# Mixture of softmaxes on one core: one reciprocal and weight product for four heads, four places for exponentials, a hand-written set of waits

## The chip, the cores and the metric

The kernel runs on one core of a Trainium2 chip. The metric is the device time of one execution in microseconds (us), lower is better. A profiled execution gives a span, from the first to the last instruction, and a trace of every instruction and every DMA packet. The engines named here are DVE (VectorE), ACT (ScalarE), POOL (GpSimd) and SP (SyncE, which only issues DMAs in this kernel). ACT can issue DMAs too. TensorE is not used.

## The reference

```python
def reference(logits, prior):            # logits [32, 128, 4, 4096], prior [32, 128, 4], float32
    prior_probs = np.exp(prior - prior.max(axis=-1, keepdims=True))
    prior_probs = prior_probs / prior_probs.sum(axis=-1, keepdims=True)
    softmax = np.exp(logits - logits.max(axis=-1, keepdims=True))
    softmax = softmax / softmax.sum(axis=-1, keepdims=True)
    return np.sum(prior_probs[..., None] * softmax, axis=2)   # [32, 128, 4096]
```

There are 4,096 rows (batch times sequence). Each has four heads of 4,096 logits. The result of a row is the sum of the four softmaxes, each weighted by the softmax of the row's four priors. 268 MB of logits are read and 67 MB of results written.

## The kernel before

The rows are cut into 32 units of 128 rows, one row per partition. A unit's logits are 128 x 4 x 4,096 float32: 8 MB in all, 64 KB in each partition. Two such buffers (`ltile`, line 72) take turns, so that unit b + 2 is loaded where unit b was. A load is issued by SP: one DMA of 8 MB for most units, four of 2 MB (one for each head) for unit 0 and the last three (lines 66 to 76).

The prologue (lines 87 to 105) loads the priors, computes their softmax with the rows along the free dimension, and transposes the weights into `pp`, which holds for each partition and unit the four weights.

The loop over units (line 119) does for each of the four heads:

- line 135, ACT: exponential of the head's 4,096 logits, with the sum along the row as a by-product (`dsum`). The exponentials go to one of two buffers, `ebuf`, which take turns; for the last two units they are written in place over the logits. No maximum is subtracted.
- line 144, DVE: reciprocal of the sum (`rden`), 128 x 1.
- head 0, line 146, DVE: `acc` = exponentials times reciprocal times weight, in one operation with two scalars.
- heads 1 to 3, line 151, POOL: `coeff` = reciprocal times weight, 128 x 1; then line 156, DVE: `acc` = exponentials times `coeff` plus `acc`. For the last head of the last unit this is done in two halves, each with its own store.

An `acc` has two buffers of its own (16 KB per partition); in the last two units it lies in the load buffer. The store of unit b - 1 is issued on ACT's queue ahead of the exponentials of unit b (line 129); the stores of the last four units go out on SP's queue after all loads (lines 163 to 168, 161). Each engine works through its own queue in order. A scheduler of the language puts in the waits between engines; a load waits until its buffer's four exponentials are done, and an exponential waits until the add that reads its `ebuf` is done.

Of the kernel before, what the change touches and what calls it, by code (L numbers as in the profile page):

```python
# [1 line left out]

# [4 lines left out]

FP32 = mybir.dt.float32
AF = mybir.ActivationFunctionType
ALU = mybir.AluOpType  # L10
AX = mybir.AxisListType


def early_first_load(nc):

    blocks = nc.main_func.blocks  # L20
    first = next(
        (b, i)
        for b in blocks[1:]
        for i in b.instructions
        if i.engine == mybir.EngineType.SP and i.opcode == "DMACopy"
    )
    block, ins = first
    assert not ins.sync_info.on_wait
    block.instructions.remove(ins)
    at = next(  # L30
        n
        for n, i in enumerate(blocks[0].instructions)
        if i.engine == mybir.EngineType.SP and i.opcode == "Drain"
    )
    blocks[0].instructions.insert(at, ins)


@with_exitstack
def kernel(
    ctx: ExitStack,  # L40
    tc: tile.TileContext,
    logits: bass.AP,
    prior: bass.AP,
    out: bass.AP,
):
    nc = tc.nc
    B, S, H, V = logits.shape
    assert prior.shape == (B, S, H)
    assert out.shape == (B, S, V)
    P = 128  # L50
    J = 2
    R = P * J
    G = B * S // R
    B = G * J
    assert G * R == B * S and G <= 32

    lg = logits.rearrange("b s h v -> (b s) h v").rearrange("(g p j) h v -> g j p h v", p=P, j=J)
    ov = out.rearrange("b s v -> (b s) v").rearrange("(g p j) v -> g j p v", p=P, j=J)
    pv = prior.rearrange("b s h -> (b s) h").rearrange("(g r) h -> g r h", r=R)

    lpool = ctx.enter_context(tc.tile_pool(name="lpool", bufs=2))
    apool = ctx.enter_context(tc.tile_pool(name="apool", bufs=2))
    cpool = ctx.enter_context(tc.tile_pool(name="cpool", bufs=1))


    def pieces(b):
        return 1 if b == 0 or b >= B - 3 else H

    ltiles = {}

    def load(b, eng=nc.sync):
        lt = lpool.tile([P, H, V], FP32, name="ltile")
        n = pieces(b)
        for h in range(0, H, n):
            eng.dma_start(out=lt[:, h : h + n], in_=lg[b // J, b % J, :, h : h + n, :])  # L75
        ltiles[b] = lt

    accs = {}

    def store(b, lo=0, hi=V, eng=nc.sync):  # L80
        eng.dma_start(out=ov[b // J, b % J, :, lo:hi], in_=accs[b][:, lo:hi])

    load(0, eng=nc.sync)
    nc.at_finalize(early_first_load)


    pr = cpool.tile([G, R, H], FP32, name="pr")
    nc.scalar.dma_start(out=pr, in_=pv)
    load(1, eng=nc.sync)
    pn = cpool.tile([32, H, R], FP32, name="pn")  # L90
    nc.gpsimd.memset(pn, 0.0)  # L91
    pmax = cpool.tile([G, R], FP32, name="pmax")
    nc.vector.reduce_max(pmax, pr, axis=AX.X)  # L93
    nc.vector.tensor_sub(pr, pr, pmax.unsqueeze(2).to_broadcast([G, R, H]))  # L94
    nc.scalar.activation(pr, pr, AF.Exp)  # L95
    nc.vector.reduce_sum(pmax, pr, axis=AX.X)  # L96
    nc.vector.reciprocal(pmax, pmax)  # L97
    nc.vector.tensor_mul(  # L98
        pn[0:G].rearrange("g h r -> g r h"), pr, pmax.unsqueeze(2).to_broadcast([G, R, H])
    )  # L100
    pq = pn.rearrange("g h (p j) -> g j h p", j=J)

    pp = cpool.tile([P, J, H, 32], FP32, name="pp")
    for t in range(P // 32):
        nc.vector.transpose(pp[32 * t : 32 * (t + 1)], pq[:, :, :, 32 * t : 32 * (t + 1)])  # L105

    NCHUNK = 2


    dsum = cpool.tile([P, B * H], FP32, name="dsum")  # L110
    rden = cpool.tile([P, B * H], FP32, name="rden")
    coeff = cpool.tile([P, B * H], FP32, name="coeff")


    ebuf = cpool.tile([P, 2, V], FP32, name="ebuf")

    exps = []

    for b in range(B):
        last = b == B - 1  # L120
        inplace = b >= B - 2
        lt = ltiles.pop(b)
        if not inplace:
            accs[b] = apool.tile([P, V], FP32, name="acc")
        else:
            accs[b] = lt[:, 0]
        acc = accs[b]
        if 0 < b < B - 3:
            store(b - 1, eng=nc.scalar)
        for h in range(H):  # L130
            split = last and h == H - 1
            i = b * H + h
            col = slice(i, i + 1)
            et = lt[:, h] if inplace else ebuf[:, h % 2]
            ex = nc.scalar.activation(et, lt[:, h], AF.Exp, accum_out=dsum[:, col])  # L135
            if h == 0:
                tc.keep_in_program_order(ex)


            if not inplace:  # L140
                if len(exps) >= 2:
                    tc.declare_no_dep(ex.ins, exps[-2], reason="covered by the sum")
                exps.append(ex.ins)
            nc.vector.reciprocal(rden[:, col], dsum[:, col])  # L144
            if h == 0:
                nc.vector.tensor_scalar(  # L146
                    out=acc, in0=et, scalar1=rden[:, col], scalar2=pp[:, b % J, h, b // J : b // J + 1],
                    op0=ALU.mult, op1=ALU.mult,
                )
                continue  # L150
            nc.gpsimd.tensor_mul(coeff[:, col], rden[:, col], pp[:, b % J, h, b // J : b // J + 1])  # L151
            n = NCHUNK if split else 1
            w = V // n
            for c in range(n):
                cs = slice(c * w, (c + 1) * w)
                nc.vector.scalar_tensor_tensor(  # L156
                    out=acc[:, cs], in0=et[:, cs], scalar=coeff[:, col], in1=acc[:, cs],
                    op0=ALU.mult, op1=ALU.add,
                )
                if split:  # L160
                    store(b, c * w, (c + 1) * w)
        if b + 2 < B:
            load(b + 2)
        if b == B - 3:
            store(b - 1)
            store(b)
        elif b == B - 2:
            store(b)


# [1 line left out]
_INS = ['logits', 'prior']  # L172
_OUTS = [((32, 128, 4096), 'float32')]


# [23 lines left out]
```

The softmax here doesn't subtract the row's maximum and nothing guards it: scores larger than these inputs give would overflow.

## Time and profile before

| What | Value |
|---|---|
| Median of 4 runs | 782.81 us (782.76 to 782.86) |
| The profiled execution | 782.86 us, span 780.7 us |
| DVE busy | 531.4 us, 68% of the span, 266 instructions |
| ACT busy | 470.2 us, 60%, 258 instructions |
| POOL busy | 19.3 us, 2%, 101 instructions |
| Exponential, line 135 | 120 + 8 of 3,608 ns |
| First head's product, line 146 | 30 + 2 of about 2,413 ns |
| Add, line 156 | 90 of 4,484 ns, and 7 in the last two units |
| Reciprocal, line 144 | 128 of 160 ns |
| Weight product on POOL, line 151 | 96 of 190 ns |
| Chain that ended last | DMA of loads 66%, ACT 14%, DVE 10% |

The page of a profile lists the busy time of each engine, the span in 40 slices, the DMA queues with the bytes they moved, the chain of work that ended last, and the costliest groups of instructions by line. A group is written with what it writes, an arrow, and what it reads. "q1" is the DMA queue that SP issues to, "q10" that of ACT, "q14" carries blocks of instructions that the engines run. Idle time of an engine that does not set the end costs nothing.

### The profile page before, as it was taken

The numbers are of one execution on the slowest core, as the hardware profiler recorded it, in microseconds if no ns is written. First come the engines' busy times: TensorE is split into PE (matmuls) and PEld (weight loads), VectorE is DVE, ScalarE is ACT, GpSimd is POOL, SyncE is SP. The second block draws the span as 40 slices with busy tenths as digits, with TensorE's granted clock in tenths as the row PEclk, the third lists the DMA queues.
The fourth block names the chain that finished last, engine by engine and source line by source line (L and its number), as shares of the span: only waits on it lengthen the run. The fifth ranks groups of instructions, "written<-read, shape, count | busy, mean of one in ns | idle before, by whom it ended". The sixth has DMA issues, their size and how long they took to land.

```text
span 780.7 us, 853 instructions
## 1 busy us (share of the span) xinstructions
DVE 531.4 (68%) x266; ACT 470.2 (60%) x258; POOL 19.3 (2%) x101
## 2 busy tenths in 40 slices
DVE  5646668656686666866667765677666776668994
ACT  4366555755557655576555765457655567558971
POOL 0000000000000000000000000000000000000000
DMA  9999999999999999999999999999999999999998
GB/s 393 430 423 463 403 470 403 466 408 422 451 415 458 408 462 406 436 438 460 413 436 447 404 459 414 452 421 452 410 458 415 453 416 421 452 413 431 429 429 357
DMA packets 11127, 335.67 MB, mean 430 GB/s; under 512 B 1248, under 2 KB 1248, under 8 KB 1264
## 3 DMA queue, kind: packets, MB, share of 16 engines
q1 hardware_dynamic: 7056, 276.83, 82.2%
q10 hardware_dynamic: 4064, 58.79, 17.6%
q14 instruction: 7, 0.06, 0.0%
HBM read 268.50 MB, written 67.11 MB: 430 GB/s over the span
## 4 chain that ended last, share of the span: by engine, by line
DMA 66%; ACT 14%; DVE 10%; issue 7%; POOL 0%; SPq 0%; DVEq 0%; POOLq 0%; ACTq 0%
DMA ltile<-in_logits_dram 66%; ACT ebuf L135 14%; DVE acc L156 9%; DVE ltile L156 1%; POOL coeff L151 0%; SPq L75 0%; DVE rden L144 0%; DVEq L194 0%; DVE ltile L146 0%; POOLq L194 0%; ACTq L135 0%
## 5 line engine op out<-in xcount | busy, mean ns | idle before, releaser
L135 ACT ACTIVATE ebuf<-ltile 128x4096 f32<-128x4096 f32 x120 | 433.0, 3608 | 281.8 <-DMA ltile<-in_logits_dram 235.1
L156 DVE SCALAR_TENSOR_TENSOR acc<-ebuf,coeff,acc 128x4096 f32<-128x4096 f32 x90 | 403.6, 4484 | 27.3 <-POOL coeff L151 27.3
L144 DVE RECIPROCAL rden<-dsum 128x1 f32<-128x1 f32 x128 | 20.4, 160 | 201.3 <-ACT ebuf L135 201.3
L146 DVE TENSOR_SCALAR acc<-ebuf,rden,pp 128x4096 f32<-128x4096 f32 x30 | 72.4, 2413 | 1.1
L151 POOL TENSOR_TENSOR coeff<-rden,pp 128x1 f32<-128x1 f32 x96 | 18.2, 190 | 746.4 <-DVE rden L144 746.4
L135 ACT ACTIVATE ltile<-ltile 128x4096 f32<-128x4096 f32 x8 | 28.9, 3609 | 4.2 <-DMA ltile<-in_logits_dram 4.2
L156 DVE SCALAR_TENSOR_TENSOR ltile<-ltile,coeff 128x4096 f32<-128x4096 f32 (+1 forms) x7 | 27.0, 3874 | 1.8 <-POOL coeff L151 1.8
L135 ACT ACTIVATION_READ_ACCUMULATOR ebuf<-ltile 128x1 f32 x120 | 22.4, 186 | 0.0
L93 DVE TENSOR_REDUCE pmax<-pr 16x256 f32<-16x1024 f32 x1 | 1.2, 1207 | 6.6 <-DMA pr<-in_prior_dram 6.6
L95 ACT ACTIVATE pr<-pr 16x1024 f32<-16x1024 f32 x1 | 1.1, 1055 | 6.6 <-DVE pr L94 6.6
L146 DVE TENSOR_SCALAR ltile<-ltile,rden,pp 128x4096 f32<-128x4096 f32 x2 | 4.8, 2414 | 0.1
L98 DVE TENSOR_TENSOR pn<-pr,pmax 16x1024 f32<-16x1024 f32 x1 | 1.9, 1943 | 0.1
L95 ACT ACT_TABLE_LOAD x1 | 1.3, 1283 | 1.2 <-PEq L183 1.2
L96 DVE TENSOR_REDUCE pmax<-pr 16x256 f32<-16x1024 f32 x1 | 1.2, 1207 | 1.1 <-ACT pr L95 1.1
L105 DVE STREAM_TRANSPOSE pp<-pn 32x256 f32<-32x256 f32 x4 | 1.7, 436 | 0.1
L97 DVE RECIPROCAL pmax<-pmax 16x256 f32<-16x256 f32 x1 | 1.7, 1741 | 0.0
L135 ACT ACTIVATION_READ_ACCUMULATOR ltile<-ltile 128x1 f32 x8 | 1.5, 187 | 0.0
L94 DVE TENSOR_TENSOR pr<-pr,pmax 16x1024 f32<-16x1024 f32 x1 | 1.2, 1211 | 0.0
L91 POOL MEMSET pn<- 32x1024 f32 x1 | 0.9, 941 | 0.3 <-POOLq L183 0.3
L183 POOL MEMSET const-float32-0.0<- 128x1 f32 x1 | 0.1, 103 | 0.2 <-issue 0.2
L183 POOL MEMSET const-bfloat16-1.0<- 128x1 bf16 x1 | 0.1, 106 | 0.0
L183 POOL MEMSET const-uint8-127<- 128x1 uint8 x1 | 0.1, 106 | 0.0
(1 smaller groups left out, 0.1 us busy)
## 6 DMA issues: line engine op xcount, KB each, us to landing
out_dram<-acc ACTq DMA_DIRECT2D x28, 2048.0 KB, 29.3
ltile<-in_logits_dram SPq DMA_DIRECT2D x16, 2048.0 KB, 20.2
out_dram<-acc SPq DMA_DIRECT2D x2, 2048.0 KB, 32.9
out_dram<-ltile SPq DMA_DIRECT2D x1, 2048.0 KB, 21.2
out_dram<-ltile SPq DMA_DIRECT2D x2, 1024.0 KB, 8.7
ltile<-in_logits_dram SPq DMA_DIRECT2D x28, 32.3
pr<-in_prior_dram ACTq DMA_DIRECT2D x1, 64.0 KB, 5.8
```

The source lines that it names most:

```text
L93: nc.vector.reduce_max(pmax, pr, axis=AX.X)
L94: nc.vector.tensor_sub(pr, pr, pmax.unsqueeze(2).to_broadcast([G, R, H]))
L95: nc.scalar.activation(pr, pr, AF.Exp)
L96: nc.vector.reduce_sum(pmax, pr, axis=AX.X)
L97: nc.vector.reciprocal(pmax, pmax)
L98: nc.vector.tensor_mul(pn[0:G].rearrange("g h r -> g r h"), pr, pmax.unsqueeze(2).to_broadcast([G, R, H]))
L105: nc.vector.transpose(pp[32 * t : 32 * (t + 1)], pq[:, :, :, 32 * t : 32 * (t + 1)])
L135: ex = nc.scalar.activation(et, lt[:, h], AF.Exp, accum_out=dsum[:, col])
L144: nc.vector.reciprocal(rden[:, col], dsum[:, col])
L146: nc.vector.tensor_scalar(out=acc, in0=et, scalar1=rden[:, col], scalar2=pp[:, b % J, h, b // J : b // J + 1], op0=ALU.mult, op1=ALU.mult,)
L151: nc.gpsimd.tensor_mul(coeff[:, col], rden[:, col], pp[:, b % J, h, b // J : b // J + 1])
L156: nc.vector.scalar_tensor_tensor(out=acc[:, cs], in0=et[:, cs], scalar=coeff[:, col], in1=acc[:, cs], op0=ALU.mult, op1=ALU.add,)
```

## The change

The loop is written anew with an order by hand, and with its waits by hand too. In each unit the four exponentials come first, then one reciprocal of 128 x 4 sums, one POOL product of 128 x 4 weights, and then the four DVE operations. In the last four units this is done for two heads at a time. The exponentials of heads 0 to 3 go to four different places: head 0 in place in the load buffer, head 1 to `ebuf1`, head 2 to `ebuf2` in PSUM, head 3 to `ebuf3`. The first head's product has one scalar, `coeff`, and no longer two. The results lie in `obuf`, two buffers as before.

The waits that `only` keeps in the loop:

- a load of unit u waits for the first DVE operation of unit u - 2 (the four pieces of a late unit: the first piece for that, the others for the exponential of their head);
- an exponential of heads 1 to 3 waits for its load and for the DVE operation of the unit before that read its buffer; the fourth, from unit 4 on, also for the store of unit u - 4;
- the reciprocal waits for the last exponential of its group; the POOL product for the reciprocal and, in the first group of a unit, for the store of unit u - 2, which read the same `obuf`;
- the first DVE operation of a group waits for the product, the others for the one before them;
- a store waits for the last add of its unit.

The store of unit u - 1 now stands on ACT's queue ahead of the fourth exponential of unit u, where it stood ahead of the first. The last four units' stores stay on SP's queue behind the loads. The prologue does what it did.

```diff
-    lpool = ctx.enter_context(tc.tile_pool(name="lpool", bufs=2))
-    apool = ctx.enter_context(tc.tile_pool(name="apool", bufs=2))
...
+    def only(ins, *keep):
+        for k in keep:
+            tc.add_manual_dep(
+                ins.ins,
+                k.ins.name,
+                mybir.DependencyInfo(mybir.DependencyClass.Sync, mybir.DependencyReason.DATA),
+                reason="all that this instruction waits for",
+            )
+        tc.declare_no_dep(
+            ins.ins,
+            group="loop",
+            keep=[k.ins for k in keep] + before.get(ins.ins.engine, []),
+            reason="covered by the waits that are kept",
+        )
...
+    ltile = cpool.tile([P, 2, H, V], FP32, name="ltile")
...
+            if u >= 2:
+                only(ld, adds[u - 2, 0] if h == 0 else exps[u - 2, h])
+            else:
+                only(ld)
...
+    def store(u, acc, eng, lo=0, hi=V):
+        st = eng.dma_start(out=ov[u // J, u % J, :, lo:hi], in_=acc[:, lo:hi])
+        stores[u] = only(st, adds[u, H - 1])
...
-    ebuf = cpool.tile([P, 2, V], FP32, name="ebuf")
+    ebuf1 = cpool.tile([P, V], FP32, name="ebuf1")
+    ebuf2 = psum.tile([P, V], FP32, name="ebuf2")
+    ebuf3 = cpool.tile([P, V], FP32, name="ebuf3")
+    obuf = cpool.tile([P, 2, V], FP32, name="obuf")
...
+        for u in range(U):
+            bufd = u < U - 2
+            lt = ltile[:, u % 2]
+            acc = obuf[:, u % 2] if bufd else lt[:, 0]
+            es = (lt[:, 0], ebuf1, ebuf2, ebuf3) if bufd else [lt[:, h] for h in range(H)]
...
+            def exp(h, *keep):
...
+                keep = (loads[u, h],) + keep
+                if bufd and h and u:
+                    keep += (adds[u - 1, h],)
+                exps[u, h] = only(ex, *keep)
+
+            def weigh(h, n, *keep):
+                rc = nc.vector.reciprocal(rden[:, u, h : h + n], dsum[:, u, h : h + n])
+                only(rc, exps[u, h + n - 1])
+                mul = nc.gpsimd.tensor_mul(
+                    coeff[:, u, h : h + n], rden[:, u, h : h + n], ppu[:, h : h + n]
+                )
+                return only(mul, rc, *keep)
+
+            def add(h, mul, lo=0, hi=V):
+                if h == 0:
+                    st = nc.vector.tensor_scalar(
+                        out=acc[:, lo:hi], in0=es[h][:, lo:hi], scalar1=coeff[:, u, h : h + 1],
+                        scalar2=None, op0=ALU.mult,
+                    )
+                    adds[u, h] = only(st, mul)
+                else:
+                    st = nc.vector.scalar_tensor_tensor(
+                        out=acc[:, lo:hi], in0=es[h][:, lo:hi], scalar=coeff[:, u, h : h + 1],
+                        in1=acc[:, lo:hi], op0=ALU.mult, op1=ALU.add,
+                    )
+                    adds[u, h] = only(st, mul, adds[u, h - 1])
+
+            free = (stores[u - 2],) if bufd and u >= 2 else ()
+
+            m = H if u < U - 4 else 2
+            for h in range(H):
+                late = h == H - 1 and 4 <= u < U - 3
+                if h == H - 1 and 0 < u < U - 3:
+                    store(u - 1, obuf[:, (u - 1) % 2], nc.scalar)
+                exp(h, *((stores[u - 4],) if late else ()))
+                if (h + 1) % m:
+                    continue
+                g = h + 1 - m
+                mul = weigh(g, m, *(free if g == 0 else ()))
+                for k in range(g, h + 1):
+                    n = 2 if u == U - 1 and k == H - 1 else 1
+                    w = V // n
+                    for c in range(n):
+                        add(k, mul, c * w, (c + 1) * w)
+                        if n > 1:
+                            store(u, acc, nc.sync, c * w, (c + 1) * w)
+            if u + 2 < U:
+                load(u + 2)
```

## The prediction

> **What bounds the kernel now.** I read the page's slices and queues first, then a table of windows over the span, then the waits, then the chain of one unit, and last the tail on the timeline.
>
> ```profile
> DMA  9999999999999999999999999999999999999998
> DMA packets 11127, 335.67 MB, mean 430 GB/s; under 512 B 1248, under 2 KB 1248, under 8 KB 1264
> q1 hardware_dynamic: 7056, 276.83, 82.2%
> q10 hardware_dynamic: 4064, 58.79, 17.6%
> q14 instruction: 7, 0.06, 0.0%
> ```
>
> The DMA engines are never under nine tenths before the last slice, and the loads (q1, with the last five stores) and the other stores (q10) fill 99.8% of 16 engines. The windows (us, busy time of DVE, ACT, POOL, clock, DMA share, GB/s) say where the rest is:
>
> ```profile
> 0.00:2.00 2.00, 0.00 (x0) 0.80 (x1) 1.15 (x5) 1.00 0.63 139
> 2.00:10.00 8.00, 2.42 (x2) 1.39 (x2) 0.00 (x0) 1.00 0.98 403
> ...
> 200.00:300.00 100.00, 68.55 (x33) 61.82 (x34) 2.40 (x13) 1.00 1.00 433
> ...
> 772.00:776.00 4.00, 0.00 (x0) 0.00 (x0) 0.00 (x0) 1.00 0.97 410
> 776.00:778.00 2.00, 0.00 (x0) 0.00 (x0) 0.00 (x0) 1.00 0.76 320
> 778.00:780.70 2.70, 0.00 (x0) 0.00 (x0) 0.00 (x0) 1.00 0.07 30
> ```
>
> Idle DMA time is 0.74 us in the first two (0.37 x 2.00), 0.16 in the next eight, 0.12 + 0.48 + 2.51 in the last nine: 4.0 us in all. Between, the transfers run at 433 GB/s whatever the engines do. The bytes are fixed, so 335.67 MB / 433 GB/s = 775.2 us is the floor; no scheduling of DVE, ACT or POOL can win more than the 4.0 us. Of these the opening 0.9 stays (the first load and the prior's load are issued as before), and the packet records put the last packet's end at 779.4 us, so that the final landing and drain, 1.3 us, stay too. What is winnable is 4.0 - 0.9 - 1.3 = 1.8 us: the uneven finish. By the same records 12 of 16 DMA engines end between 777.3 and 777.6 us and the last at 779.4, so 1.8 to 1.9 us after most.
>
> ```profile
> ACT ebuf L135 <- DMA ltile<-in_logits_dram: 235.1, 28, 15.4
> DVE rden L144 <- ACT ebuf L135: 201.3, 57, 13.2
> ACT ebuf L135 <- DVE acc L156: 44.6, 32, 1.4
> ```
>
> ACT waits 235.1 us for loads, which is the bound seen from the engine; the 44.6 us for a free ebuf and all POOL round trips lie under it. One middle unit (13) by the chain of waits (start, us, what), then its store and the next unit on the timeline:
>
> ```profile
> 332.47 7.32 ACT ebuf L135 x4
> 348.32 0.20 ACT ebuf L135
> 348.54 32.29 DMA ltile<-in_logits_dram
> ```
> ```profile
> 354.52 0.34 ACTq L81 DMA_DIRECT2D out_dram<-acc  x1
> 356.65 3.62 ACT L135 ACTIVATE ebuf<-ltile 128x4096 f32<-128x4096 f32 x1 [8.14 <-DMA ltile<-in_logits_dram]
> ```
>
> Call T the start of a unit's first exponential. Units follow at 356.65 - 332.47 = 24.18 us. The load two units on goes out at T + 16.07, 8.1 us before the next unit's data are in, so the load queue has work; the store goes out at T + 22.05.
>
> **The change part by part.** *Reciprocals and weights.* 128 reciprocals of 160 ns become 36, 96 POOL products of 190 ns become 36: 92 x 0.16 = 14.7 us of DVE and 60 x 0.19 = 11.4 us of POOL go, all under the transfers. The wider forms (128x4) have no row; the 16x256 reciprocal at 1,741 ns bounds them above, 160 ns below; I take the lower, being nearer. Worth nothing while the DMA is full; were it not, a unit would lose or win at most 1.6 us.
>
> *Three exponential tiles, one in PSUM, one in place.* ACT no longer stalls 1.42 us a unit: four exponentials take 3.62 + 3 x 3.60 + 0.17 = 14.6 us. A 128x4096 exponential into PSUM and an add that reads PSUM have no row. For the add the same operation from SBUF (4,484 ns) is nearest; below lies the 2,412 ns of TENSOR_SCALAR, above I allow twice 4,484. Taken: 4,484. The exponential in place has a row (3,609, against 3,608); into PSUM I take 3.61 us, with 1.8 and 7.2 as half and double. At 7.2 the load of the next paragraph leaves 3.6 us later, still 3.1 ahead; at 8.97 for the add the store leaves up to 1.6 us later. Both stay hidden in the middle; the tail is rival B.
>
> *The load's release.* Load u+2 now waits for the first add of unit u, which waits for all four sums: 14.6 + 0.03 + 0.47 (reciprocal start to add start, 50.81 to 51.28) + 2.41 = T + 17.5, so 1.4 us later than now and 6.7 us before the next unit.
>
> *The store's place.* The store of u-1 stands before the fourth exponential of u on ACT's queue: T + 3.62 + 2 x 3.60 + 0.1 = T + 10.95 of the next unit, that is 35.1 us after its own T instead of 22.05, 13 us later. Behind it on ACT waits only that fourth exponential. The adds of u-1 end at 14.6 + 0.5 + 2.41 + 3 x 4.48 = T + 31.0, before 35.1, so it hardly waits. But POOL's product of u now waits for the landing of store u-2 (obuf has two halves). Issue to landing is 29.3 us (median), so T - 24.18 + 10.95 + 29.3 = T + 16.1, 1.3 us after the sums would allow; the add then ends and the load goes out at T + 16.1 + 0.2 + 2.4 = 18.7, 5.5 us ahead. Behind that product on POOL is nothing until the next unit; on DVE the four adds, which then end at T + 32.2, still under 35.1. The work that hides all this is the other queue: in steady state a store is always in transit, and if the load queue runs dry for a moment the store goes faster. What one queue loses the other gets. Cost 0.
>
> A rule bears on this. The Trainium skill, "DMA: Bandwidth & Descriptors" (Queues, rings and completion order), says that a DMA engine takes packets from its queues in turn. One 16 KB store packet per 64 KB load packet would make a store of 8 packets per engine last as long as a load, a whole period of 24.2 us, however early it is issued. That speaks against putting it later. By the rule its landing would be 24.2 us plus the way in and out, at best T + 11, the product would not wait and the lead would be 6.7 us; by the row above it is 5.5.
>
> *The start.* Load 2 went out at 28.08 us; now after the four sums of unit 0 and its first add, about 30.5 us by the same durations. Load 1 occupies the queue until 42.5 (packet records): cost 0. The first store goes from 34.1 to about 54 us; until then the loads have the engines alone.
>
> *The tail.* Here a term is on the path.
>
> ```profile
> 760.38 3.62 ACT L135 ACTIVATE ltile<-ltile 128x4096 f32<-128x4096 f32 x1 [1.16 <-DMA ltile<-in_logits_dram]
> 761.46 4.48 DVE L156 SCALAR_TENSOR_TENSOR ltile<-ltile,coeff 128x4096 f32<-128x4096 f32 x1 [0.30 <-POOL coeff L151]
> 766.32 4.62 DVE L156 SCALAR_TENSOR_TENSOR ltile<-ltile,coeff 128x2048 f32<-128x2048 f32 x2 [0.30 <-POOL coeff L151]
> ```
>
> Now the third head's add runs beside the last exponential. With one weight op for two heads it waits for that exponential's sum: 764.09 + 0.47 = 764.6, add to 769.1, halves to 771.4 and 773.7, against 768.6 and 770.9: 2.75 us later. The packet records show the halves' first packets at 772.44 and 775.28, since earlier stores stand before them in the queue. So 1.0 us and 1.5 us remain from issue to transfer. From issue to first packet the very first load took 1.0 us, the prior's load, behind other packets, 3.8. At 1.0 the queue never runs dry; at 3.8 it is dry for 2.8 us on most DMA engines, but the slowest is 1.9 us behind and feels 0.9. Cost 0 to 0.9; I take 0, the first load's row being the nearer one (same engine and queue).
>
> *Fewer instructions.* The seven q14 packets are instruction blocks. The records show them at 147 to 750 us, each delaying its DMA engine by about 0.65 us; the engine that ends last collected several. Instructions go from 853 to about 853 - 92 - 60 = 701, so perhaps 5.8 blocks rather than 7. Worth 0 (another engine) to 1.8 us (all gone); taken 0.4.
>
> Sum: 780.7 - 0.4 = 780.3 us span. The profiled run took 782.86 for its 780.7, so 2.16 lie around the span: 782.46; the median is 0.05 under that run, hence 782.4.
>
> **Rivals.** *A, slower: the landing of a store closes a loop.* Store u-2 at T + 10.95, landing L later, product and add 2.7, then an unqueued load (8.39 MB and a store's 2.10 MB at 433 GB/s, 24.2 us, and 0.7 to land) over three periods: 3P = 10.95 + L + 2.7 + 24.9. It decides from P = 24.18, that is L = 34.0; each us beyond costs 28/3 = 9.3 us, so 791.7 at L = 35. For it: landings now range from 13.6 to 33.5 us. Against: a load queue that runs dry speeds the store up. *B, slower at the end:* if an add from PSUM takes 8.97 us, units 28 and 29 push DVE back 9 us, the halves end near 777.4 and 779.7, and with 1.0 us to start, 2.4 us for 1 MB and 1.3 to drain the span is 784.4: 786.6. For it: no PSUM row; against: the 4,484 ns add has no fast form to lose. *C, faster:* the uneven finish goes wholly, -1.8: 781.0. For it: fewer instruction blocks; against: some must remain, on some DMA engine.
>
> **How the numbers follow.** A change under 0.2% (1.6 us) I count as none, since that is about what this kernel's measurement tells apart. Forecast 0.80, with own range 781.2 (most of C's gain) to 783.7 (0.9 in the tail). A 0.08, B 0.06, C beyond 0.2% 0.06. The range 781.0 to 784.0 leaves A, B and part of C out. Faster 0.06, same 0.80, slower 0.14.
>
> **What would show it.** DMA share 1.00 and 433 GB/s in every window from 42 to 770 us proves the core of it; ACT's wait for loads grows by the 44.6 us it no longer waits for DVE; stores leave some 13 us later; q14 counts fewer packets; the last half's add ends near 773.7. Wrong: a window in the middle under 1.00 (A), adds from PSUM well over 4.5 us (B).

## The result, and the profile after

The changed kernel takes 781.53 us (median of 41 runs) against 782.69 us (61 runs of the kernel before), a ratio of 0.9987 with a 95% interval of 0.9983 to 0.9992. It is 1.16 us faster, within the 0.2% that the prediction counted as no change. The medians of the spans are 779.8 and 780.6 us, so 0.8 us were won inside the span. The other 0.36 us lie outside it: 1.77 us against about 2.13 us.

First the same page lines of the changed kernel: engines, DMA slices and queues.

```profile
DVE 520.9 (67%) x174; ACT 467.4 (60%) x258; POOL 8.3 (1%) x41
...
DMA  9999999999999999999999999999999999999998
...
q1 hardware_dynamic: 7056, 276.83, 82.3%
q10 hardware_dynamic: 4064, 58.79, 17.6%
q14 instruction: 5, 0.04, 0.0%
```

DVE was busy 10.5 us less and POOL 11.0, and nothing of it shows in the DMA lines: the transfers fill the span as before. Only q14, the blocks of instructions, went from 7 packets to 5. The windows (us, busy DVE, ACT, POOL, clock, DMA share, GB/s) of the changed kernel say the same:

```profile
0.00:2.00 2.00, 0.00 (x0) 0.81 (x1) 1.15 (x5) 1.00 0.60 131
...
200.00:300.00 100.00, 66.64 (x22) 58.02 (x32) 0.97 (x5) 1.00 1.00 433
...
600.00:700.00 100.00, 67.28 (x21) 61.37 (x35) 0.80 (x4) 1.00 0.99 429
...
772.00:776.00 4.00, 0.71 (x1) 0.00 (x0) 0.00 (x0) 1.00 0.95 399
776.00:778.00 2.00, 0.00 (x0) 0.00 (x0) 0.00 (x0) 1.00 0.68 287
778.00:779.70 1.70, 0.00 (x0) 0.00 (x0) 0.00 (x0) 1.00 0.01 5
```

433 GB/s in the middle, as before. The difference is in the last row: before, a few DMA engines still moved bytes after 778 us (share 0.07), now almost none (0.01). By the packet records the last packet ends at 778.37 us instead of 779.40, 1.03 us earlier, which is the whole difference of the two profiled spans (779.7 and 780.7). The waits of the changed kernel:

```profile
POOL coeff L167 <- DVE rden L165: 754.6, 36, 30.0
ACT ltile L156 <- DMA ltile<-in_logits_dram: 285.0, 36, 15.6
DVE rden L165 <- ACT ebuf L156: 224.4, 29, 13.7
```

ACT hardly stalls for an `ebuf` any more (1.2 us in all, 44.6 before) and waits some 50 us longer for its loads (285.0 against 235.1). A stall off the path was turned into waiting for the bound. One middle unit of the changed kernel on the timeline (start, length, what), T = 354.76:

```profile
347.98 13.53 DVE L180 SCALAR_TENSOR_TENSOR obuf<-ebuf,coeff,obuf 128x4096 f32<-128x4096 f32 x3
354.76 3.62 ACT L156 ACTIVATE ltile<-ltile 128x4096 f32<-128x4096 f32 x1 [9.69 <-DMA ltile<-in_logits_dram]
...
358.37 3.60 ACT L156 ACTIVATE ebuf<-ltile 128x4096 f32<-128x4096 f32 x1
361.54 0.34 ACTq L110 DMA_DIRECT2D out_dram<-obuf  x1
...
361.97 3.57 ACT L156 ACTIVATE ebuf<-ltile 128x4096 f32<-128x4096 f32 x1
...
369.30 0.18 DVE L165 RECIPROCAL rden<-dsum 128x4 f32<-128x4 f32 x1 [7.79 <-ACT ebuf L156]
...
372.17 24.48 SPq L97 DMA_DIRECT2D ltile<-in_logits_dram  x2
...
378.91 3.62 ACT L156 ACTIVATE ltile<-ltile 128x4096 f32<-128x4096 f32 x1 [9.65 <-DMA ltile<-in_logits_dram]
```

The load goes out at T + 17.4, 6.7 us ahead of the next unit, as worked out. The store goes out at T + 6.8, when the adds of the unit before have just ended (347.98 + 13.53) and the second exponential still runs, and not at T + 10.95.

The tail of the changed kernel:

```profile
759.36 3.62 ACT L156 ACTIVATE ltile<-ltile 128x4096 f32<-128x4096 f32 x1 [1.18 <-DMA ltile<-in_logits_dram]
...
763.57 9.13 DVE L180 SCALAR_TENSOR_TENSOR ltile<-ltile,coeff 128x4096 f32<-128x4096 f32 x3 [0.31 <-POOL coeff L167]
```

The three DVE operations are the third head's add and the two halves, ending at 772.70. From the last exponential's start that is 13.34 us, where the prediction had 773.7 - 760.4 = 13.3; the exponential itself starts 1.0 us earlier (760.38 before), because its load lands earlier. The slowest DMA engine lags 0.6 us less here, as the table below shows; where the other 0.4 us come from was not traced.

### The profile page after: what moved, and what is told of

It is laid out like the page before. It is cut to its first block, busy times and chain, and to the rows that moved or that the text cites. A ratio compares the mean times of both kernels' runs of the same rounds, so it can differ in the third digit from the quotient of the medians.

```text
span 779.7 us, 670 instructions
## 1 busy us (share of the span) xinstructions
DVE 520.9 (67%) x174; ACT 467.4 (60%) x258; POOL 8.3 (1%) x41
## 4 chain that ended last, share of the span: by engine, by line
DMA 62%; ACT 26%; DVE 8%; issue 2%; POOL 0%; DVEq 0%; SPq 0%; POOLq 0%; ACTq 0%
DMA ltile<-in_logits_dram 62%; ACT ebuf L156 19%; ACT ltile L156 7%; DVE obuf L174 5%; DVE obuf L180 2%; DVE ltile L180 1%; POOL coeff L167 0%; DVE rden L165 0%; DVEq L237 0%; SPq L97 0%; POOLq L237 0%; ACTq L110 0%
## 5 line engine op out<-in xcount | busy, mean ns | idle before, releaser
L180 DVE SCALAR_TENSOR_TENSOR obuf<-ebuf,coeff,obuf 128x4096 f32<-128x4096 f32 x90 | 403.6, 4484 | 3.8 <-POOL coeff L167 0.6
L156 ACT ACTIVATE ebuf<-ltile 128x4096 f32<-128x4096 f32 x90 | 322.9, 3589 | 2.9 <-DMA ltile<-in_logits_dram 1.7
L156 ACT ACTIVATE ltile<-ltile 128x4096 f32<-128x4096 f32 x38 | 137.4, 3616 | 285.0 <-DMA ltile<-in_logits_dram 285.0
L165 DVE RECIPROCAL rden<-dsum 128x4 f32<-128x4 f32 (+1 forms) x36 | 6.3, 174 | 229.3 <-ACT ebuf L156 224.4
L174 DVE TENSOR_SCALAR obuf<-ltile,coeff 128x4096 f32<-128x4096 f32 x30 | 70.6, 2353 | 9.4 <-POOL coeff L167 9.4
L156 ACT ACTIVATION_READ_ACCUMULATOR ebuf<-ltile 128x1 f32 x90 | 16.8, 186 | 0.0
L167 POOL TENSOR_TENSOR coeff<-rden,pp 128x4 f32<-128x4 f32 (+1 forms) x36 | 7.2, 199 | 754.6 <-DVE rden L165 754.6
L156 ACT ACTIVATION_READ_ACCUMULATOR ltile<-ltile 128x1 f32 x38 | 7.1, 186 | 0.0
L174 DVE TENSOR_SCALAR ltile<-ltile,coeff 128x4096 f32<-128x4096 f32 x2 | 4.7, 2352 | 0.6 <-POOL coeff L167 0.6
## 6 DMA issues: line engine op xcount, KB each, us to landing
out_dram<-obuf ACTq DMA_DIRECT2D x28, 2048.0 KB, 29.4
```

The lines of the kernel that those rows point to most:

```text
L156: ex = nc.scalar.activation(es[h], lt[:, h], AF.Exp, accum_out=dsum[:, u, h : h + 1])
L165: rc = nc.vector.reciprocal(rden[:, u, h : h + n], dsum[:, u, h : h + n])
L167: mul = nc.gpsimd.tensor_mul(coeff[:, u, h : h + n], rden[:, u, h : h + n], ppu[:, h : h + n])
L174: st = nc.vector.tensor_scalar(out=acc[:, lo:hi], in0=es[h][:, lo:hi], scalar1=coeff[:, u, h : h + 1], scalar2=None, op0=ALU.mult,)
L180: st = nc.vector.scalar_tensor_tensor(out=acc[:, lo:hi], in0=es[h][:, lo:hi], scalar=coeff[:, u, h : h + 1], in1=acc[:, lo:hi], op0=ALU.mu ...
```

## The experiments

All of them change the changed kernel. Ratios are to the kernel before, run beside them.

**Is it the instruction blocks? Four kernels with more instructions.** m1 takes the weights head by head again:

```diff
-            m = H if u < U - 4 else 2
+            m = 1
...
-                only(ld, adds[u - 2, 0] if h == 0 else exps[u - 2, h])
+                only(ld, *((adds[u - 2, 0], exps[u - 2, h + n - 1]) if h == 0 else (exps[u - 2, h],)))
```

> One reciprocal and one POOL product per head again (92 more of each), all else as in the changed kernel; a load then waits for the first add and the last exponential of its buffer. Theory 'blocks' (the gain is the more even finish of the DMA engines, because fewer instruction blocks are fetched): about 850 instructions as in the kernel before, so q14 moves 7 packets again instead of 5, and the time goes back to 782.2 to 782.8. Rival 'order' (the gain is the new order of stores and loads and the stalls that went): 781.3 to 781.7, as the order stays.

The three others add memsets at the end of a unit (3 on DVE and 2 on POOL in pad_both; 20 on POOL in pad_pool20; 12 on DVE in pad_dve12):

```diff
+    spare = cpool.tile([P, 1024], FP32, name="spare")
...
+            for k in range(12):
+                at = 0 + 12 * u + k
+                only(nc.vector.memset(spare[:, at : at + 1], 0.0))
```

> The changed kernel with three more 128x1 memsets on DVE and two more on POOL in each unit, on a tile that nothing reads: 155 more instructions and nothing else. Theory 'blocks': q14 back to 6 or 7 packets, 782.0 to 782.8. Rival 'order': 781.3 to 781.7.

> The changed kernel with twenty more 128x1 memsets on POOL in each unit, 640 in all, on a tile that nothing reads; POOL is 1% busy, so its time is free. Theory 'blocks': about five more q14 packets, each delaying its DMA engine by 0.65 us; between 781.5 (on engines that end early) and 784.8 (all on the engine that ends last). Rival 'order': 781.3 to 781.7.

> The changed kernel with twelve more 128x1 memsets on DVE in each unit, 384 in all, on a tile that nothing reads; some 1.2 us of DVE in a unit in which it idles 8. Theory 'blocks': about three more q14 packets, 781.5 to 783.5 by the DMA engine that they fall on. Rival 'order': 781.3 to 781.7.

| Kernel | Instructions | q14 packets | Lag of the slowest DMA engine at the last 64 KB packets (about 690 us), us | Span profiled, us | Time, us (ratio, interval) |
|---|---|---|---|---|---|
| before | 853 | 7 | 1.83 | 780.7 | 782.69 |
| changed | 670 | 5 | 1.26 | 779.7 | 781.53 (0.9987, 0.9983 to 0.9992) |
| m1 | 854 | 6 | 2.67 | 780.7 | 782.06 (0.9991, 0.9982 to 1.0) |
| pad_both | 830 | 6 | 1.38 | 779.8 | 781.69 (0.9987, 0.9978 to 0.9996) |
| pad_pool20 | 1310 | 10 | 2.90 | 782.1 | 784.02 (1.0016, 1.0007 to 1.0025) |
| pad_dve12 | 1054 | 8 | 3.72 | 782.2 | 783.95 (1.0014, 1.0006 to 1.0023) |

The lag is read from the packet records: the start of the last of the 16 engines on the last round of 64 KB load packets, less that of the first. m1's lag and profiled span come from an execution of 782.52 us.

m1 lies in neither band, the ranges that the theory and its rival gave. The median of its spans is 780.3 us, between 779.8 of the changed kernel and 780.6 before, so 0.5 of the 0.8 us came back with the instructions; the 0.36 us outside the span did not. pad_both, at 781.69 us with 6 packets, missed the band of the blocks and lies in its rival's. pad_pool20 is inside the band of the blocks, pad_dve12 0.45 us above it. In these two, instructions that nobody waits for, on engines that idle in every unit, cost 2.4 to 2.5 us, so the theory holds in kind. The number of packets alone does not fix the time: eight in pad_dve12 cost as much as ten in pad_pool20.

What counts is which DMA engine they fall on. Almost every packet in the records starts within 5 ns of the end of another, so packets can be followed one behind the other: they fall into 16 rows with 224 load packets each, one row for each DMA engine. A block sets its row back by 0.5 to 0.9 us: 309 ns are its own, and the packet behind it takes longer, up to 3,064 ns for a load packet instead of 2,418. In pad_dve12 a DVE unit has 17 instructions, and the blocks at 84, 264, 449 and 629 us lie 180 to 185 us apart, 7.5 units, or 128 instructions. All four lie in one row and set it back by 0.84 to 0.92 us each; that row ends at 780.84 us, the other 15 by 778.95. In pad_pool20 five blocks (75, 227, 373, 518 and 643 us) lie in one row and set it back by 0.5 to 0.6 us each. So, as far as these records show, the blocks of one compute engine come through one DMA engine, and the DMA engine that is set back most ends last.

The same reading explains the lag of the two kernels. Before, the last row starts its last load packet 1.6 us behind the median row, with two steps of 0.8 us at 147 and 486 us. In the changed kernel it is 1.0 us, with two steps of 0.55 us at 148 and 511 us; a single step of 0.84 us (194 us) falls on another row.

In pad_dve12 the late engine also delays the last load's landing, and with it the last adds. The timeline of pad_dve12 (its line numbers are one higher for the added tile), and one of its windows:

```profile
761.83 3.62 ACT L157 ACTIVATE ltile<-ltile 128x4096 f32<-128x4096 f32 x1 [1.14 <-DMA ltile<-in_logits_dram]
...
766.05 9.13 DVE L181 SCALAR_TENSOR_TENSOR ltile<-ltile,coeff 128x4096 f32<-128x4096 f32 x3 [0.31 <-POOL coeff L168]
```
```profile
772.00:776.00 4.00, 3.33 (x14) 0.00 (x0) 0.00 (x0) 1.00 0.64 262
```

The last load lands 2.5 us later than in the changed kernel, and now the store queue does run dry: DMA share 0.64 in the window from 772 to 776 us, where the changed kernel has 0.95. The lag of one engine thus became the end of all.

**When does the load's release matter?** rel1 and rel2 wait for the second or third DVE operation instead of the first (rel2: index 2):

```diff
-                only(ld, adds[u - 2, 0] if h == 0 else exps[u - 2, h])
+                only(ld, adds[u - 2, 1] if h == 0 else exps[u - 2, h])
```

> The changed kernel, but a load waits for the second DVE operation of its buffer's unit instead of the first, so it goes out 4.5 us later, at T + 22 of a period of 24.2, about 1.5 us before the load queue is empty. Theory 'the queues cover each other' (what one queue loses the other gets): 781.3 to 782.0. Rival 'the release of the load is on the path': every unit later by up to 1 us, 785 to 810.

> The same with the third DVE operation: the load goes out at T + 26.5, after the next unit's data are in, so the load queue is dry for about 3 us in every unit. Theory 'the queues cover each other': the store's 4.8 us of transfer fill the gap, 781.5 to 790. Rival 'a dry load queue is idle time': two periods last 26.5 + 1 to start + 24.2 + 0.7 to land = 52.4 us, 26.2 a unit, 2.0 x 29 more, about 840.

Measured 794.1 us (1.0141, 1.0123 to 1.016) and 855.39 us (1.0925, 1.0909 to 1.0942). The theory fell, and its rival held in kind: rel1 is inside the rival's band, rel2 15 us above its 840. The windows from 100 to 700 us, in order the changed kernel, rel1 and rel2:

```profile
100.00:700.00 600.00, 399.38 (x125) 357.29 (x197) 5.01 (x25) 1.00 1.00 432
```
```profile
100.00:700.00 600.00, 387.77 (x123) 354.11 (x196) 5.01 (x25) 1.00 1.00 427
```
```profile
100.00:700.00 600.00, 351.83 (x111) 329.38 (x182) 4.42 (x22) 1.00 0.96 390
```

rel1 is the instructive one: the DMA share stays 1.00 while the rate falls. A load is issued only 1.2 to 1.9 us before the load ahead of it ends (5.6 us or more in the changed kernel), and its first packet starts 1.7 to 3.1 us after the issue. So the load queue is dry for 0.5 to 1.4 us in most units. The DMA engines are not idle, since the store's packets then follow one another without a gap; but the load packets last longer. A 64 KB load packet takes 2,418 ns in the changed kernel almost without exception (longest 2,955). In rel1 it takes up to 3,282 ns, and the excess over 2,418 sums to 11.5 us for each of the 16 engines (0.5 in the changed kernel), nearly the whole difference of the profiled spans, 791.3 and 779.7 us. Between 100 and 680 us it is 9.4 us; in rel2 it is 32.0 us there, and idle time comes on top.

The longer packets are not simply the first ones behind the gap. Of rel1's 9.4 us, 0.3 lie on the first of the eight packets that a load has on each DMA engine, and 9.0 on the last four, where the store's packets stand between them again. In rel2, 12.8 of the 32.0 us lie on the first packet and 11.7 on the last. Why they are slower was not tried.

**When does the place of the store matter?** st1 and st2 put it ahead of the second and third exponential:

```diff
-                if h == H - 1 and 0 < u < U - 3:
+                if h == 1 and 0 < u < U - 3:
```

> The changed kernel with the store of unit u - 1 ahead of the second exponential of unit u on ACT's queue instead of the fourth. It waits for the last add of u - 1, and the second exponential waits behind it: a loop through ACT and DVE of three exponentials, the weights and four DVE operations, 10.8 + 0.7 + 2.4 + 13.5 = 27.4 us a unit, more than the 24.2 of the transfers. Theory (a place on ACT's queue costs what stands behind it): 865 to 885. Rival (the DMA bound hides it): 781.3 to 783.

> The changed kernel with the store of u - 1 ahead of the third exponential of unit u. The trace of the changed kernel shows the store issued at T + 6.8, as its last add ends, while the third exponential starts at T + 7.2: so the third exponential has 0.4 us to spare, and its place should cost nothing: 781.3 to 782. Rival (the loop of ACT and DVE, 23.8 us, plus 0.3 for the issue, is too near to 24.2): 784 to 800.

st1 took 872.37 us (one run), within its band. Its waits:

```profile
ACT ebuf L156 <- DVE obuf L180: 343.0, 27, 13.3
...
ACT ltile L156 <- DMA ltile<-in_logits_dram: 32.2, 7, 15.6
```

ACT now waits 343.0 us behind stores that wait for DVE, and only 32.2 us for loads: the bound has moved from the transfers to the loop through ACT and DVE. st2 took 781.82 us (0.9989, 0.998 to 0.9998): the third exponential has the 0.4 us to spare.

**The tail.** tail4 gives the last four units one weight op each, tail1 gives the last unit four:

```diff
-            m = H if u < U - 4 else 2
+            m = H
```
```diff
-            m = H if u < U - 4 else 2
+            m = H if u < U - 4 else 2 if u < U - 1 else 1
```

> The changed kernel with one reciprocal and product for four heads in the last four units too. The last unit's four DVE operations then all follow its last exponential: the last halves are added by 777.2 and 779.5 us instead of 770.4 and 772.7. Theory (earlier stores cover the tail only to about 774): the DMA queue runs dry, the end follows the adds, 0.35 to issue, 1.0 to start, 2.4 of transfer, 1.3 to drain: span 784 to 785, time 785.5 to 786.5. Rival (the tail is hidden anyway): 781.3 to 782.

> The changed kernel with one reciprocal and product for each head in the last unit alone: the last halves are added some 2 us earlier. Theory (the earlier stores still cover the tail in the changed kernel): 781.3 to 781.8, no gain. Rival (the 1.8 us that the last adds lost are on the path): 780 to 781.

tail4 took 786.72 us (1.0052, 1.0039 to 1.0064), 5.2 us more than the changed kernel, 0.2 over the expected band. Its windows:

```profile
768.00:772.00 4.00, 3.96 (x2) 0.00 (x0) 0.00 (x0) 1.00 1.03 442
772.00:776.00 4.00, 3.96 (x2) 0.00 (x0) 0.00 (x0) 1.00 0.07 29
776.00:780.00 4.00, 3.84 (x2) 0.00 (x0) 0.00 (x0) 1.00 0.39 164
```

The queue runs empty at 772 us and waits for the first half. tail1 took 781.95 us (0.9991, 0.9982 to 1.0), 0.4 over the changed kernel and 0.15 over its band. Its median span is 779.8 us, equal to the changed kernel's, though in its profile the last adds end at 771.14 us instead of 772.70: in the span the tail is hidden. The 0.4 lie outside the span (2.12 us, like the kernel before); what sets that part was not found.

**All stores through SP's queue.**

```diff
-                    store(u - 1, obuf[:, (u - 1) % 2], nc.scalar)
+                    store(u - 1, obuf[:, (u - 1) % 2], nc.sync)
```

> The changed kernel with all stores on SP's queue, each between the loads, so that loads and stores go through one queue one after the other and ACT has 28 instructions fewer. The store of u - 1 goes out at T + 6.8 of unit u and stands behind load u + 1; load u + 2 stands behind it. Nothing runs dry: 24.2 us a unit as before. Theory 'blocks': one block fewer for ACT at best, one more for SP at worst, 781.0 to 781.8. Rival 'two queues are needed' (a store between two loads leaves a gap): 0.5 us or more a unit, 796 or more.

784.4 us (1.0023, 1.0014 to 1.0032), between the two bands: neither theory foresaw it. The middle runs at 432 GB/s as in the changed kernel, so stores between loads leave no gap. But the slowest DMA engine is 3.7 us behind at the last load packets, with only five q14 packets. That lag grew in the first 300 us, in some seven steps of which at most two fall on a block (165 and 192 us). Blocks are therefore not the only source of an uneven finish.

## Why the prediction was right

Its forecast was 782.4 us, no change, and the range 781.0 to 784.0 us; the kernel came to 781.53. What it rested on, the floor, held. Two small terms were off, by 0.5 us in the span and 0.39 around it, and both on the fast side; that the sum still lies in the range, 0.5 us above its lower end, owes something to luck.

- *The floor.* Right. Every window from 42 to 770 us stayed at 429 GB/s or more (429 between 600 and 740 us, where the kernel before has 432 and 431). The share of 0.99 between 600 and 700 us is under the 1.00 that the prediction named as a sign of Rival A, but by the packet records no DMA engine idles in that window. What ACT no longer stalls went into waiting for loads.
- *Fewer instructions.* The mechanism was named, and its size was off: 0.4 us were taken out of 0 to 1.8, and the span gave 0.8 (medians) to 1.0 (profiles). The step scaled the number of blocks with the number of instructions, which came to 670 and not 701: 31 semaphore waits went too, 129 before and 98 after. The runs show that it is the delay on the worst DMA engine that matters, 1.6 us before and 1.0 after.
- *Around the span.* 2.16 us were carried over unchanged and became 1.77. That this part could change was missing altogether, and it is a third of the gain of the medians. Why is open: among these kernels there are just two levels, about 2.12 (the kernel before and tail1) and about 1.78 (all others).
- *The store's place.* Wrong in detail. The prediction let the store wait for the third exponential to end, T + 10.95. ACT's queue issued it at T + 6.8, the moment the last add ended, before the third exponential started; against the store's old time of T + 22.05 of its own unit it went out 8.9 us later, and not 13. By the same step's landing row (29.4 us in the page of after) it lands at T + 12.0 of the next unit, so that POOL's product never waited for it: all 754.6 us of POOL's waits are for the reciprocal. The rule from the Trainium skill, "DMA: Bandwidth & Descriptors" (Queues, rings and completion order), had led to the same lead of 6.7 us, by another way: it made the landing earlier, not the issue. The trace agrees with the rule: in both kernels, between 100 and 680 us, 2,672 of 3,056 store packets, seven of eight, stand directly behind a load packet of the same DMA engine.
- *Why the load's release costs nothing.* The result was right, one reason was wrong. "What one queue loses the other gets" holds for the time of the DMA engines, which do not idle in rel1, but not for the rate: rel1 lost 12.6 us with its load queue dry for about a microsecond a unit. The release is free because the queue never goes dry, with 6.7 us of lead; 4.5 us less is already too little. Rival A did not come about: in the changed kernel and in rel1 alike POOL waited for the reciprocal alone (754.6 and 766.2 us), never for the landing of a store. What the rivals lacked is a release of the load that comes too late by itself; the changed kernel lies 4.5 us or less from there.
- *PSUM.* Right: the adds, a third of which read PSUM, take 4,484 ns on average, as before. The exponential into PSUM takes some 3.56 us against 3.60.
- *The tail.* Right: the 13.3 us from the last exponential to the last add came out as worked, and the halves' packets started at 772.20 and 774.90, in time. tail1 shows that it is hidden, tail4 where it stops being so. The 1.0 us from issue to first packet held: in pad_pool20 the first half's add ends at 772.8 (765.99 + 4.48 + 2.3) and its packets start at 773.72.

## What to carry to other kernels

In a kernel whose DMA share is 1.00 from end to end, add up the idle DMA time of the windows first: it was 4.0 us here, and no work on the compute engines could win more. What such a change can still lose is the lead of the loads, so measure by how much a release may slip before the load queue is empty (here by less than 4.5 us); a share of 1.00 does not prove full speed, look at the GB/s beside it. The end is set by the slowest of the 16 DMA engines, so instructions that cost no time on their engine can cost some through the blocks in which they are fetched.

## What the runs showed of the hardware

- A block of instructions (8 KB, 309 ns in the records) sets the DMA engine that carries it back by 0.5 to 0.9 us, since the load packet behind it lasts 2,635 to 3,064 ns instead of 2,418. The blocks of DVE in pad_dve12 came every 128 instructions, all on one DMA engine, which was 3.6 us behind the median engine at about 690 us.
- Where the load queue runs dry for a short time in each unit (rel1), 64 KB load packets last up to 3,282 ns instead of 2,418, with all DMA engines busy; most of the excess lies on the last four of a load's eight packets on an engine, not on the first.
- ACT's queue issues a DMA whose wait is met while an earlier exponential is still running: at 361.54 us, inside the exponential from 358.37 to 361.97, and ahead of the third one, which stands before it in the program and starts at 361.97.
- Loads and stores in one queue (sp_stores) moved as fast as in two, but their 16 engines drifted 3.7 us apart, against 1.3 (read at about 690 us).
